# GLA level products over the later halves of the queries, packed two blocks to a bank, with the diagonal apart

## The chip, the cores and the metric

The kernel runs on one core of a Trainium2 chip. The metric is device time in microseconds of one execution. In the profile PE is TensorE's matmul, PEld its weight load, DVE is VectorE, ACT ScalarE, POOL GpSimd, and SP the queue that starts most DMA transfers.

## The reference

A two-layer decoder trunk on 512 tokens of width 1024, all in float32. Each layer has three mixers on one projection (differential attention, a short convolution, gated linear attention), an output projection, and a layer of 16384 single-neuron experts. The change concerns the gated linear attention (GLA): 4 heads with 32 key and 64 value channels, in chunks of 64 tokens.

```python
def step(state, inp):                      # one chunk of 64 tokens
    qi, ki, vi, ai = inp
    b = lax.cumsum(ai, axis=2)
    diff = b[:, :, :, None, :] - b[:, :, None, :, :]
    decay = jnp.exp(jnp.where(causal[:, :, None], diff, -jnp.inf))
    attn = jnp.sum(qi[:, :, :, None, :] * ki[:, :, None, :, :] * decay, axis=-1)
    o = jnp.einsum('bhij,bhje->bhie', attn, vi) + jnp.einsum('bhid,bhde->bhie', qi * jnp.exp(b), state)
    b_last = b[:, :, -1:, :]
    state = jnp.exp(b_last[:, :, 0, :, None]) * state + jnp.einsum(
        'bhjd,bhje->bhde', ki * jnp.exp(b_last - b), vi)
    return state, o
```

The decay differs for each key channel, so `attn` is not one plain product of queries and keys.

## The kernel before

Each layer runs `mixer` and then the expert stage. `mixer` projects the normalized tokens with slabs of 256 columns of w_in. A slab is loaded in four pieces (wraw, L242), split by ScalarE into a rounded part wh (L80) and by VectorE into the rest wl (L81), and multiplied in three passes (L75 to L77) into psp. Slabs are double-buffered. While TensorE works through the slabs of the attention's queries, keys and values, `mixer` draws pieces of `gla` from a generator: `fill(n)` advances it until the costs that it yields add up to n. For the queries and keys each slab has also a rotation on VectorE (the rope: rm and qkn, L413 to L418) and transposes on TensorE (rtr, L422). The framework then orders the instructions of each engine by its own list scheduling, and each engine executes its list in that order.

`gla` works with 128 partitions (4 heads of 32 key channels) and 512 tokens. After the cumulative decay b, the masked matrix `at` (keys in partitions; block, head and query along the row) is built in seven levels (`level`, L527 to L547). Level s = 32, 16, 8, 4, 2, 1 covers the pairs whose key lies in the earlier and whose query in the later half of the same block of 2s tokens. With r the decay at the middle of that block, d is exp(r - b) in the earlier half and exp(b - r) in the later one (ld, L534 to L536). Keys are multiplied by d (ks, L539), and so are the queries of all tokens, spread out by head in qbm so that one product forms all four heads (qs, L540). For each block of 128 tokens TensorE forms a product of 128 keys with 4 x 128 queries (pst, L545), and VectorE copies from it the entries that the mask of that level selects (L547). The level s = 0 is the diagonal, with plain gk and qbm. Half of each product's columns, those of queries in earlier halves, are never selected.

Between levels, `gla` transposes the decayed keys (trk, L562), forms the chunk updates (psu, L572) and the states S on VectorE (L574 to L578). At the end it forms qe (L590), which shares its buffer with qs, and for each block the outputs pg from states (L596, L597) and from `at` (L599), normalizes them and transposes them (htr, L479). The attention's scores are pss (L438).

PSUM pool psA has four banks, used by pst, rtr and trk among others.

Of the kernel before, what the change touches and what calls it, by code (L numbers as in the profile page):

```python
# [7 lines left out]
F32 = mybir.dt.float32  # L8
# [4 lines left out]
U32 = mybir.dt.uint32  # L13
AF = mybir.ActivationFunctionType
OP = mybir.AluOpType
# [4 lines left out]
P = 128  # L20
T = 512
TB = T // P
# [37 lines left out]
def bc(ap, pattern):  # L60
    return bass.AP(tensor=ap.tensor, offset=ap.offset, ap=[ap.ap[0]] + pattern)


class K:
# [418 lines left out]
    def gla(self, L, gq, gk, gv, sg, lr, mgh, mgl, gp):  # L483
        nc, tc, ins = self.nc, self.tc, self.ins
# [5 lines left out]
        ggain = gp.tile([P, 1], F32, name="ggain")  # L490
        for i in range(2):
            nc.sync.dma_start(ggain[64 * i:64 * i + 64], ins["gla_norm"][L].rearrange("(p o) -> p o", o=1))
        lmask = gp.tile([P, 7, P], U32, name="lmask")
        nc.sync.dma_start(lmask, ins["c_levels"].rearrange("l p i -> p l i"))
        bdmask = gp.tile([P, 256], F32, name="bdmask")
        nc.gpsimd.memset(bdmask, 0.0)
        qbm = gp.tile([P, TB, 4, P], F32, name="qbm")
        nc.gpsimd.memset(qbm, 0.0)
        for h in range(4):
            r = slice(32 * h, 32 * h + 32)  # L500
            nc.gpsimd.memset(bdmask[r, 64 * h:64 * h + 64], 1.0)
            nc.scalar.copy(qbm[r, :, h], gq[r].rearrange("p (n i) -> p n i", i=P))
        reset = gp.tile([P, T], F32, tag="ld", name="reset", bufs=2)
        nc.gpsimd.memset(reset, 1.0)
        nc.gpsimd.memset(reset.rearrange("p (n c) -> p n c", c=C)[:, :, 0:1], 0.0)
# [1 line left out]
        def tmp(name):  # L507
            return gp.tile([P, T], F32, tag="tmp", name=name, bufs=2)
# [10 lines left out]
        b = gp.tile([P, T], F32, name="b")  # L519
# [4 lines left out]
        at = gp.tile([P, TB, 4, P], F32, name="at")  # L524
        nc.gpsimd.memset(at, 0.0)

        def level(li, s):  # L527
            if s:
                n = T // (2 * s)
                d = gp.tile([P, T], F32, tag="ld", name="ld", bufs=2)  # L530
                dv = d.rearrange("p (n two s) -> p n two s", two=2, s=s)
                bv = b.rearrange("p (n two s) -> p n two s", two=2, s=s)
                r = bc(b[:, s - 1:T], [[2 * s, n], [0, s]])
                nc.vector.tensor_tensor(dv[:, :, 0], r, bv[:, :, 0], op=OP.subtract)  # L534
                nc.vector.tensor_tensor(dv[:, :, 1], bv[:, :, 1], r, op=OP.subtract)
                nc.scalar.activation(d, d, AF.Exp)  # L536
                ks = gp.tile([P, T], F32, tag="ks", name="ks", bufs=2)
                qs = gp.tile([P, TB, 4, P], F32, tag="qs", name="qs", bufs=1)
                nc.vector.tensor_tensor(ks, gk, d, op=OP.mult)  # L539
                nc.vector.tensor_tensor(qs, qbm, bc(d, [[P, TB], [0, 4], [1, P]]), op=OP.mult)  # L540
            else:
                ks, qs = gk, qbm
            for tb in range(TB):
                pst = self.psA.tile([P, 4, P], F32, tag="a", name="pst")
                nc.tensor.matmul(pst, ks[:, tb * P:tb * P + P], qs[:, tb].rearrange("p h i -> p (h i)"),  # L545
                                 start=True, stop=True)
                nc.vector.copy_predicated(at[:, tb], bc(lmask[:, li], [[0, 4], [1, P]]), pst)  # L547

        levels = [(li, s) for li, s in enumerate((32, 16, 8, 4, 2, 1, 0))]
        level(*levels[0])  # L550
        yield 5

# [4 lines left out]
                                op=OP.subtract)  # L557
# [6 lines left out]
        nc.scalar.copy(kdT, trk)  # L564
        yield 3
        level(*levels[1])
        yield 6
        S = gp.tile([P, NC - 1, 256], F32, name="S")
# [11 lines left out]
        for lv in levels[2:]:  # L580
            level(*lv)
            yield 6
        self.tap("at", at)
        eb = tmp("eb")
        nc.scalar.activation(eb, b, AF.Exp)
        qe = gp.tile([P, 2, T], F32, tag="qs", name="qe", bufs=1)
        nc.gpsimd.memset(qe, 0.0)
        for i in range(2):
            sl = lambda t: t.rearrange("p (n two c) -> p n two c", two=2, c=C)[:, :, i]
# [2 lines left out]
        for tb in range(TB):  # L592
            pg = self.psB.tile([P, 256], F32, tag="b", name="pg")
            t0 = tb * P
# [3 lines left out]
            for h in range(4):  # L598
                nc.tensor.matmul(pg[:, 64 * h:64 * h + 64], at[:, tb, h], gv[:, tb, 64 * h:64 * h + 64],  # L599
                                 start=False, stop=(h == 3))  # L600
# [407 lines left out]
def lay_out(inputs):  # L1008
    import numpy as np

    a = {n: np.asarray(v) for n, v in inputs.items()}
    L = DEPTH
    r = {}
    r["x"] = a["x"].reshape(T, D)
    r["positions"] = a["positions"].reshape(T)
    for n in ("norm_mix", "norm_ffn", "w_in", "lam_q1", "lam_k1", "lam_q2", "lam_k2", "diff_norm", "gla_w_gate2", "gla_b_gate", "gla_norm",
              "w_out", "norm_final"):
        r[n] = a[n]
    r["conv_w"] = a["conv_w"].reshape(L, 3, 2, P).transpose(0, 3, 2, 1)
    r["peer_w_q"] = a["peer_w_q"].reshape(L, KD, P, 16, P).transpose(0, 3, 2, 1, 4)  # L1020
    for n in ("peer_keys1", "peer_keys2"):
        r[n] = a[n].transpose(0, 2, 1)
    r["peer_u"] = a["peer_u"].reshape(L, NCH, P, KD, P).transpose(0, 1, 4, 3, 2)
    r["u_rows"] = a["peer_u"].reshape(L * NCH * P, D)
    r["v_rows"] = a["peer_v"].reshape(L * NCH * P, D)
    r["c_ident"] = np.eye(P, dtype=np.float32)
    j, i = np.arange(P)[:, None], np.arange(P)[None, :]
    xr = j ^ i
    r["c_levels"] = np.stack([((xr >= s) & (xr < 2 * s) & (i > j)) if s else (xr == 0)
                              for s in (32, 16, 8, 4, 2, 1, 0)]).astype(np.uint32)  # L1030
    return {n: np.ascontiguousarray(v) for n, v in r.items()}


# [14 lines left out]
```

## Time and profile before

| | us |
|---|---|
| median of 3 runs (lowest, highest) | 3073.7 (3073.36, 3074.85) |
| the profiled execution | 3068.26 |
| its span, first to last instruction | 3066.5 |
| TensorE busy in the span | 2996.6 |
| VectorE busy | 2470.3 |
| GLA of layer 0, from psz to the first attention score | 128.80 |
| GLA of layer 1, the same | 128.60 |

Runs are compared by the time of the whole execution; the profile gives one execution's span, 1.8 us shorter than its time. A busy TensorE may be one whose passes overlap: an instruction's recorded length includes time in which the next one already runs, so the pace is the distance between two starts.

### The profile page before, as it was taken

To read this page: it belongs to the slowest core of one execution; us is meant where nothing else is said; L and a number is where in the kernel's file an instruction comes from. 1 tells how busy PE (TensorE), PEld (TensorE's weight loads), DVE (VectorE), ACT (ScalarE), POOL (GpSimd) and SP (SyncE) were. 2 spreads that over 40 slices of the span, in tenths; PEclk is the share of its full clock that TensorE was granted. 3 is DMA by queue.
4 is the path that set the end of the run, shared out by engine and by line. 5 is a ranking of instruction groups with operands and counts; after the bars stand their busy time and mean duration, and the time that the engine had idled before them with its cause. 6 is when DMAs were issued, how large, how long until landed. Compare 5 with 4: busy or idle time off the path is not lost.

```text
span 3066.5 us, 45595 instructions
## 1 busy us (share of the span) xinstructions
PE 2996.6 (98%) x16742; PEld 2657.9 (87%) x16742; DVE 2470.3 (81%) x5079; ACT 1268.5 (41%) x1874; POOL 739.7 (24%) x543
## 2 busy tenths in 40 slices
PE   8999999999999999999999999999999999999998
PEld 7777889999999998788878788899998999988886
DVE  5777999987778887877766769999878877878777
ACT  5244346556333333333352433465553333323333
POOL 0000000222455544322100000002225555543221
PEclk9999999999999999999999999999999999999999
DMA  4112238799998888999722122478999888889996
GB/s 123 56 45 91 89 122 263 260 316 334 338 333 324 322 325 307 357 338 334 275 76 69 59 72 90 155 246 287 310 343 340 321 326 331 331 306 350 334 344 232
DMA packets 335664, 757.03 MB, mean 247 GB/s; under 512 B 30000, under 2 KB 192208, under 8 KB 331344
## 3 DMA queue, kind: packets, MB, share of 16 engines
q1 hardware_dynamic: 141904, 407.00, 37.1%
q0 software_dynamic: 73728, 268.47, 24.5%
q10 hardware_dynamic: 119808, 78.66, 8.2%
q8 instruction: 131, 2.15, 0.3%
q14 instruction: 93, 0.76, 0.1%
HBM read 673.28 MB, written 80.74 MB: 246 GB/s over the span
## 4 chain that ended last, share of the span: by engine, by line
PE 74%; issue 7%; DVE 7%; POOL 4%; DMA 3%; ACT 3%; ACTq 1%; SPq 0%; POOLq 0%; DVEq 0%
PE pv L77 9%; PE pv L75 9%; PE pv L76 9%; PE psh L75 8%; PE psh L77 8%; PE psh L76 8%; POOL row L715 4%; PE psp L77 2%; PE psp L76 2%; PE psp L75 2%; DMA row<-in_v_rows,idx 2%; PE psq L76 2%; PE psq L77 2%; PE psq L75 2%; PE pst L545 1%
## 5 line engine op out<-in xcount | busy, mean ns | idle before, releaser
L715 POOL DMA_INDIRECT row<-in_u_rows,idx x256 | 390.6, 1526 | 1315.9 <-DVE si L873 669.5
L75 PE MATMUL psh<-ahi,uh 128*128 128x384 f32 x2048 | 694.7, 339 | 10.3 <-ACT ht L645 10.3
L77 PE MATMUL psh<-ahi,ul 128*128 128x384 f32 x2048 | 689.6, 337 | 6.6 <-DVE ul L631 6.6
L76 PE MATMUL psh<-alo,uh 128*128 128x384 f32 x2048 | 688.8, 336 | 0.0
L75 PE MATMUL pv<-vh,wh 128*128 128x512 f32 x1536 | 598.1, 390 | 8.1 <-ACT wh L815 8.1
L77 PE MATMUL pv<-vh,wl 128*128 128x512 f32 x1536 | 601.2, 392 | 0.0
L76 PE MATMUL pv<-vl,wh 128*128 128x512 f32 x1536 | 600.3, 391 | 0.0
L715 POOL DMA_INDIRECT row<-in_v_rows,idx x256 | 331.5, 1295 | 601.5 <-DVE yacc L732 565.7
L630 ACT CAST uh<-uraw 128x1024 fp32r<-128x1024 f32 x288 | 302.5, 1053 | 322.0 <-PE psh L76 156.1
L631 DVE TENSOR_TENSOR ul<-uraw,uh 128x1024 fp32r<-128x1024 f32 x288 | 350.4, 1220 | 99.3 <-ACT uh L630 87.9
L75 PEld LDWEIGHTS psh<-ahi,uh 128*128 128x128 f32 x2048 | 387.0, 189 | 16.4 <-ACT ht L645 12.2
L77 PEld LDWEIGHTS psh<-ahi,ul 128*128 128x128 f32 x2048 | 386.8, 189 | 7.2 <-DVE ul L631 7.2
L76 PEld LDWEIGHTS psh<-alo,uh 128*128 128x128 f32 x2048 | 387.3, 189 | 4.1
L801 DVE TENSOR_TENSOR vl<-vraw,vh 128x1024 fp32r<-128x1024 f32 x256 | 312.6, 1221 | 83.2 <-issue 64.5
L645 ACT ACTIVATE ht<-psh 128x384 f32<-128x384 f32 x256 | 125.3, 489 | 612.4 <-PE psh L77 605.5
L75 PEld LDWEIGHTS pv<-vh,wh 128*128 128x128 f32 x1536 | 288.7, 188 | 67.5 <-ACT wh L815 10.5
L77 PEld LDWEIGHTS pv<-vh,wl 128*128 128x128 f32 x1536 | 289.0, 188 | 62.6 <-DVE wl L801 1.9
L76 PEld LDWEIGHTS pv<-vl,wh 128*128 128x128 f32 x1536 | 289.1, 188 | 59.4 <-DVE vl L801 1.0
L732 DVE SCALAR_TENSOR_TENSOR yacc<-row,wk,yacc 128x1024 f32<-128x1024 f32 x254 | 325.7, 1282 | 10.9 <-DMA row<-in_v_rows,idx 9.3
L723 DVE SCALAR_TENSOR_TENSOR gscr<-row,xg 128x1024 f32<-128x1024 f32 x256 | 312.4, 1220 | 13.2 <-DMA row<-in_u_rows,idx 11.6
L815 ACT CAST wh<-ht 128x384 fp32r<-128x384 f32 x256 | 130.7, 510 | 385.0 <-PE pv L76 229.5
L806 ACT CAST vh<-vraw 128x1024 fp32r<-128x1024 f32 x256 | 268.7, 1050 | 25.3 <-DMA vraw<-in_v_rows 24.5
(285 smaller groups left out, 4451.2 us busy)
## 6 DMA issues: line engine op xcount, KB each, us to landing
uraw<-in_peer_u SPq DMA_DIRECT2D x256, 512.0 KB
vraw<-in_v_rows SPq DMA_DIRECT2D x256, 512.0 KB
G<-stg ACTq DMA_DIRECT2D x48, 1024.0 KB
g<-G SPq DMA_DIRECT2D x32, 1536.0 KB
H<-ht ACTq DMA_DIRECT2D x144, 192.0 KB
ht<-H SPq DMA_DIRECT2D x144, 192.0 KB
wraw<-in_w_in SPq DMA_DIRECT2D x96, 256.0 KB
uraw<-in_peer_w_q SPq DMA_DIRECT2D x32, 512.0 KB
```

Source lines behind the costliest of these rows:

```text
L75: mm(ps, ah, bh, start=first, stop=False)
L76: mm(ps, ah, bl, start=False, stop=False)
L77: mm(ps, al, bh, start=False, stop=last)
L630: pin(nc.scalar.copy(hi, src))
L631: self.last = pin(nc.vector.tensor_tensor(lo, src, hi.bitcast(F32), op=OP.subtract))
L645: pin(nc.scalar.activation(hs[c], ps, AF.Gelu))
L715: nc.gpsimd.indirect_dma_start(out=r, out_offset=None, in_=ins[name], in_offset=bass.IndirectOffsetOnAxis(ap=idx[:, k:k + 1], axis=0))
L723: nc.vector.scalar_tensor_tensor(sc, r, 1.0, xg, op0=OP.mult, op1=OP.mult, accum_out=hd[:, k:k + 1])
L732: nc.vector.scalar_tensor_tensor(yacc, r, wk[:, k:k + 1], yacc, op0=OP.mult, op1=OP.add)
L801: self.last = pin(nc.vector.tensor_tensor(lo, src, hi.bitcast(F32), op=OP.subtract))
L806: pin(nc.scalar.copy(vh[c], vs[c]))
L815: pin(nc.scalar.copy(wh[c], hs[c]))
```

## The change

`level` now multiplies d only into the queries of the later halves: qs has 4 x 256 elements instead of 4 x 512 and two buffers. Each product has 4 x 64 columns, and two blocks share one bank of PSUM, from which one copy writes the later halves of both blocks into `at`; the masks hold only those columns. The level s = 0 is gone. In its place `diagonal` multiplies gq by gk on VectorE (qk), sums over each head's channels with four products with hsel, a matrix of zeros and ones with four columns (dots), and copies these sums, repeated along the row, into `at` where dmask selects the diagonal. It yields 3 instead of the 6 of a level, so the pieces of `gla` behind it are drawn one slab earlier. qe takes the new buffer form of qs.

```diff
-        lmask = gp.tile([P, 7, P], U32, name="lmask")
+        lmask = gp.tile([P, 6, P // 2], U32, name="lmask")
         nc.sync.dma_start(lmask, ins["c_levels"].rearrange("l p i -> p l i"))
+        dmask = gp.tile([P, P], U32, name="dmask")
+        nc.sync.dma_start(dmask, ins["c_diag"])
+        hsel = gp.tile([P, 4], F32, name="hsel")
+        nc.gpsimd.memset(hsel, 0.0)
...
-        qbm = gp.tile([P, TB, 4, P], F32, name="qbm")
+        qbm = gp.tile([P, 4, T], F32, name="qbm")
...
-            nc.scalar.copy(qbm[r, :, h], gq[r].rearrange("p (n i) -> p n i", i=P))
+            nc.gpsimd.memset(hsel[r, h:h + 1], 1.0)
+            nc.scalar.copy(qbm[r, h], gq[r])
...
-                qs = gp.tile([P, TB, 4, P], F32, tag="qs", name="qs", bufs=1)
-                nc.vector.tensor_tensor(ks, gk, d, op=OP.mult)
-                nc.vector.tensor_tensor(qs, qbm, bc(d, [[P, TB], [0, 4], [1, P]]), op=OP.mult)
-            else:
-                ks, qs = gk, qbm
+            qs = gp.tile([P, 4, T // 2], F32, tag="qs", name="qs", bufs=2)
+            nc.vector.tensor_tensor(ks, gk, d, op=OP.mult)
+            nc.vector.tensor_tensor(qs.rearrange("p h (n s) -> p h n s", s=s),
+                                    qbm.rearrange("p h (n two s) -> p h n two s", two=2, s=s)[:, :, :, 1],
+                                    bc(d[:, s:T], [[0, 4], [2 * s, n], [1, s]]), op=OP.mult)
+            m = P // (2 * s)
+            for t0 in range(0, TB, 2):
+                pst = self.psA.tile([P, 8, P // 2], F32, tag="a", name="pst")
+                for i in range(2):
+                    tb = t0 + i
+                    nc.tensor.matmul(pst[:, 4 * i:4 * i + 4], ks[:, tb * P:tb * P + P],
+                                     qs[:, :, tb * 64:tb * 64 + 64], start=True, stop=True)
+                nc.vector.copy_predicated(
+                    at[:, t0:t0 + 2].rearrange("p b h (n two s) -> p (b h) n two s", two=2, s=s)[:, :, :, 1],
+                    bc(lmask[:, li], [[0, 8], [s, m], [1, s]]), pst.rearrange("p g (n s) -> p g n s", s=s))
+
+        def diagonal():
+            qk = tmp("qk")
+            nc.vector.tensor_tensor(qk, gq, gk, op=OP.mult)
+            dots = self.psA.tile([P, TB, 4], F32, tag="a", name="dots")
             for tb in range(TB):
-                pst = self.psA.tile([P, 4, P], F32, tag="a", name="pst")
-                nc.tensor.matmul(pst, ks[:, tb * P:tb * P + P], qs[:, tb].rearrange("p h i -> p (h i)"),
-                                 start=True, stop=True)
-                nc.vector.copy_predicated(at[:, tb], bc(lmask[:, li], [[0, 4], [1, P]]), pst)
-
-        levels = [(li, s) for li, s in enumerate((32, 16, 8, 4, 2, 1, 0))]
+                nc.tensor.matmul(dots[:, tb], qk[:, tb * P:tb * P + P], hsel, start=True, stop=True)
+            for tb in range(TB):
+                nc.vector.copy_predicated(at[:, tb], bc(dmask, [[0, 4], [1, P]]), bc(dots[:, tb], [[1, 4], [0, P]]))
+
+        levels = [(li, s) for li, s in enumerate((32, 16, 8, 4, 2, 1))]
...
+        diagonal()
+        yield 3
...
-        qe = gp.tile([P, 2, T], F32, tag="qs", name="qe", bufs=1)
+        qe = gp.tile([P, 2, T], F32, tag="qs", name="qe", bufs=2)
```

The scheduler places some instructions elsewhere. TensorE's list differs from row 360 to row 1058 of layer 0 and in the same part of layer 1, and nowhere else; it has 17488 rows before and after. A row here is one line of an engine's list, in which equal neighbours are joined.

TensorE, levels s = 8 and 4 in layer 0 before (rows 477 to 481):

```order
L422 MATMUL rtr<-ident,qkn 128x128 x4
L545 MATMUL pst<-qs,ks 128x512
L572 MATMUL psu<-gv,kdT 128x256
L545 MATMUL pst<-qs,ks 128x512 x3
L77 MATMUL psp<-wh,alo 128x256
```

and the same place after (rows 478 to 482):

```order
L422 MATMUL rtr<-ident,qkn 128x128 x4
L552 MATMUL pst<-qs,ks 128x256 x2
L590 MATMUL psu<-gv,kdT 128x256
L552 MATMUL pst<-qs,ks 128x256 x6
L77 MATMUL psp<-wh,alo 128x256
```

Level s = 8 stood here alone, with s = 4 36 rows of psp later; now both stand together. The first level stands behind 89 rows of psp, counted from psz (row 270), where it stood behind 98, and the rows between it and the next rtr changed with it.

TensorE, the end of the levels before (rows 686 to 690), where the second pst is the diagonal:

```order
L422 MATMUL rtr<-ident,qkn 128x128 x4
L545 MATMUL pst<-qs,ks 128x512 x4
L545 MATMUL pst<-qbm,gk 128x512 x4
L76 MATMUL psp<-wl,ahi 128x256
L77 MATMUL psp<-wh,alo 128x256
```

and after (rows 684 to 688):

```order
L422 MATMUL rtr<-ident,qkn 128x128 x4
L552 MATMUL pst<-qs,ks 128x256 x4
L563 MATMUL dots<-hsel,qk 128x4 x4
L76 MATMUL psp<-wl,ahi 128x256
L77 MATMUL psp<-wh,alo 128x256
```

Behind these, 83 rows of psp stood before the first block's pg (L599 reads `at`); now 13 stand before it.

VectorE between the first half of the second slab's rope (qkn) and what precedes it, before (rows 176 to 187):

```order
L540 TENSOR_TENSOR qs<-qbm,ld 128x2048
L578 SCALAR_TENSOR_TENSOR S<-S,dec,um 128x256
L534 TENSOR_TENSOR ld<-b 128x64x4
L535 TENSOR_TENSOR ld<-b 128x64x4
L413 TENSOR_TENSOR rm<-qkn,cos 128x64
L414 TENSOR_TENSOR rm<-qkn,sin 128x64
L415 TENSOR_TENSOR rm<-qkn,sin 128x64
L416 TENSOR_TENSOR rm<-qkn,cos 128x64
L417 TENSOR_TENSOR qkn<-rm 128x8x8
L418 TENSOR_TENSOR qkn<-rm 128x8x8
L539 TENSOR_TENSOR ks<-gk,ld 128x512
L81 TENSOR_TENSOR wl<-wraw,wh 128x512 x3
```

and after, the rows ahead of that rope, which begins at row 181 (rows 170 to 180):

```order
L554 COPY_PREDICATED at<-lmask,pst 128x32x16
L544 TENSOR_TENSOR qs<-qbm,ld 128x1024
L554 COPY_PREDICATED at<-lmask,pst 128x32x16
L592 TENSOR_TENSOR S<-psu,bdmask 128x256
L595 TENSOR_TENSOR um<-psu,bdmask 128x256
L543 TENSOR_TENSOR ks<-gk,ld 128x512
L596 SCALAR_TENSOR_TENSOR S<-S,dec,um 128x256
L544 TENSOR_TENSOR qs<-qbm,ld 128x1024
L595 TENSOR_TENSOR um<-psu,bdmask 128x256
L81 TENSOR_TENSOR wl<-wraw,wh 128x512
L596 SCALAR_TENSOR_TENSOR S<-S,dec,um 128x256
```

Two qs of later levels and the first weight splits (wl) now stand ahead of that rope, where before the splits stood behind it.

## Rows read from the trace of the kernel before

**Rows 1.** The page, parts 1 and 4: busy time of each engine, and the chain by engine.
```profile
PE 2996.6 (98%) x16742; PEld 2657.9 (87%) x16742; DVE 2470.3 (81%) x5079; ACT 1268.5 (41%) x1874; POOL 739.7 (24%) x543
PE 74%; issue 7%; DVE 7%; POOL 4%; DMA 3%; ACT 3%; ACTq 1%; SPq 0%; POOLq 0%; DVEq 0%
```

**Rows 2.** Windows: length, then busy us (instructions) of PE, PEld, DVE, ACT, POOL; PEclk.
```profile
59.28:188.08 128.80, 124.03 (x795) 101.84 (x795) 89.08 (x214) 43.98 (x78) 2.80 (x3) 1.00 0.20 58
188.08:245.00 56.92, 55.48 (x282) 40.09 (x281) 46.80 (x144) 32.75 (x88) 0.00 (x0) 1.00 0.20 70
1582.00:1710.60 128.60, 124.06 (x795) 101.86 (x794) 88.94 (x214) 44.17 (x78) 2.82 (x3) 1.00 0.20 58
```

**Rows 3.** Waits of PE in 59.28:188.08: us in total, times, longest.
```profile
PE pst L545 <- DVE qs L540: 2.0, 1, 2.0
PE htr L479 <- DVE ho L471: 1.8, 2, 1.3
PE rtr L422 <- ACT wh L80: 0.4, 2, 0.2
PE rtr L422 <- DVE qkn L418: 0.2, 1, 0.2
```

**Rows 4.** Tile pst: instructions of both layers, ns min/median/max.
```profile
L545 PE MATMUL pst<-qs,ks x96: 592/592/697, 74.1 to 1662.5; 128*128 128x512 f32 x96
L545 PE MATMUL pst<-qbm,gk x16: 592/592/593, 140.3 to 1666.0; 128*128 128x512 f32 x16
L547 DVE COPY_PREDICATED at<-lmask,pst x56: 709/729/751, 75.2 to 1666.7; 128x512 f32<-128x512 uint32 x56
```

**Rows 5.** The chain, layer 0: start us, us, what (x instructions).
```profile
120.55 3.44 PE pst L545 x8
...
137.02 6.87 PE pst L545 x16
...
161.29 0.43 PE pg L596 x2
161.73 0.43 PE pg L597 x2
162.16 0.85 PE pg L599 x8
```

**Rows 6.** PE in order of time at the first level: start, us, instruction.
```profile
60.55 0.28 PE L76 MATMUL psp<-wl,ahi 128*128 128x256 f32 x1
...
71.81 0.28 PE L76 MATMUL psp<-wl,ahi 128*128 128x256 f32 x1
74.05 3.70 PE L545 MATMUL pst<-qs,ks 128*128 128x512 f32 x8 [1.96 <-DVE qs L540]
77.59 1.04 PE L422 MATMUL rtr<-ident,qkn 128*128 128x128 f32 x8
```

**Rows 7.** The chain at the first level, DVE pieces: start us, us between two starts.
```profile
69.91 0.14 DVE rm L414
71.20 0.60 DVE ks L539
71.79 2.20 DVE qs L540
...
74.60 0.34 DVE ld L534
...
76.18 0.65 DVE at L547
```

**Rows 8.** Line L535: DVE, all six levels of both layers, ns min/median/max.
```profile
L535 DVE TENSOR_TENSOR ld<-b x12: 409/417/436, 69.5 to 1637.7; 128x256 f32<-128x256 f32 x12
```

**Rows 9.** Tiles lmask and qe: the load on SP's queue, and POOL in order of time.
```profile
L494 SPq DMA_DIRECT2D lmask<-in_c_levels x2: 586/590/594, 17.2 to 1537.4; - x2
...
140.52 0.95 POOL L587 MEMSET qe<- 128x1024 f32 x1 [132.73 <-PE pst L545]
```

More of the change, by code (lines that the diff above doesn't have):

```diff
@@ L527, in level @@
         def level(li, s):
[L528 to L537, printed above, removed]
-                qs = gp.tile([P, TB, 4, P], F32, tag="qs", name="qs", bufs=1)
-                nc.vector.tensor_tensor(ks, gk, d, op=OP.mult)
-                nc.vector.tensor_tensor(qs, qbm, bc(d, [[P, TB], [0, 4], [1, P]]), op=OP.mult)
-            else:
-                ks, qs = gk, qbm
@@ L543, in level @@
-            for tb in range(TB):
-                pst = self.psA.tile([P, 4, P], F32, tag="a", name="pst")
-                nc.tensor.matmul(pst, ks[:, tb * P:tb * P + P], qs[:, tb].rearrange("p h i -> p (h i)"),
-                                 start=True, stop=True)
-                nc.vector.copy_predicated(at[:, tb], bc(lmask[:, li], [[0, 4], [1, P]]), pst)
-        levels = [(li, s) for li, s in enumerate((32, 16, 8, 4, 2, 1, 0))]
+            n = T // (2 * s)
+            halves = lambda t: t.rearrange("p (n two s) -> p n two s", two=2, s=s)
@@ new lines, in level @@
+            d = gp.tile([P, T], F32, tag="ld", name="ld", bufs=2)
+            dv, bv = halves(d), halves(b)
+            r = bc(b[:, s - 1:T], [[2 * s, n], [0, s]])
+            nc.vector.tensor_tensor(dv[:, :, 0], r, bv[:, :, 0], op=OP.subtract)
+            nc.vector.tensor_tensor(dv[:, :, 1], bv[:, :, 1], r, op=OP.subtract)
+            nc.scalar.activation(d, d, AF.Exp)
+            ks = gp.tile([P, T], F32, tag="ks", name="ks", bufs=2)
+            qs = gp.tile([P, 4, T // 2], F32, tag="qs", name="qs", bufs=2)
@@ L1028, in lay_out @@
     xr = j ^ i
-    r["c_levels"] = np.stack([((xr >= s) & (xr < 2 * s) & (i > j)) if s else (xr == 0)
-                              for s in (32, 16, 8, 4, 2, 1, 0)]).astype(np.uint32)
+    r["c_levels"] = np.stack([((xr >= s) & (xr < 2 * s) & (i > j))[:, (i[0] & s) > 0]
+                              for s in (32, 16, 8, 4, 2, 1)]).astype(np.uint32)
+    r["c_diag"] = (xr == 0).astype(np.uint32)
     return {n: np.ascontiguousarray(v) for n, v in r.items()}
```

## The prediction

> **What bounds the kernel now.** I read the page first. TensorE is busy for 98% of the span and carries 74% of the chain, VectorE 81% and 7% [rows 1]. The change touches only the gated linear attention (GLA), which each layer runs once, so I next took the stretch from its first product (psz) to the first attention score: 128.80 us in layer 0, 128.60 us in layer 1, with TensorE busy 124.03 and 124.06 us, VectorE 89.08, ScalarE 43.98, GpSimd 2.80 [rows 2]. TensorE leaves only 4.8 us there. The waits say the same: 4.4 us in all, the largest the 2.0 us before the first level product, which waits for qs [rows 3]. So in this stage time is TensorE's work plus a few short waits, and removed TensorE work should come off the end, provided that the others keep up.
>
> **What one product costs.** A fp32 product stands in the trace as two passes: 48 products of levels 0 to 5 (both layers) are 96 instructions, the 8 of the diagonal 16, and each is recorded with 592 ns [rows 4]. That length overlaps with the next pass, so I price by the distance from start to start, which the chain gives: 8 passes in 3.44 us and 16 in 6.87 us, 0.43 us for a pass over 512 columns. The passes of pg over 256 columns take 0.43 us for two, 0.215 each, and those over 64 columns 0.85 us for eight, 0.106 each [rows 5]. From 512 to 256 columns the price halves exactly; below that a floor near 0.106 us shows.
>
> **The change, TensorE.** Before, a layer issues 7 x 4 = 28 products, 56 passes x 0.43 = 24.1 us. After: 6 levels x 4 products x 2 passes = 48 passes of 256 columns x 0.215 = 10.3 us; and 4 diagonal products with 4 moving columns, 8 passes for which no row exists. Their lower bound is nothing, the nearest row is the 64-column pass, 0.106 us, so 0.85 us; the upper bound is the 256-column pass, 1.7 us. I take 0.85. Sum 11.2 us, so **12.9 us less per layer**, 25.8 us in both.
>
> The moving operand is now four runs of 64 columns and the masked half of each block. No row has that form; if it cost as much as an unbroken 512-column pass there would be only the diagonal's gain, and if it is as pg's, the full one. I take pg's, since it has the same width and type.
>
> The Trainium skill, "TensorE: Matmul & The Clock Gate", section "Back-to-back issue gap", gives a sustained 81 ns for 128 columns and 131 ns for 512, so that a quarter of the columns still costs 62%. On a line through both, a half costs 75%, an estimate from the page: 48 passes would take 15.4 us and the gain would be 7.9 us per layer, 16 us in all. The rows of this trace differ from it: 0.43 and 0.215 us [rows 5].
>
> **VectorE.** The copies fall from 28 to 16 of 512 elements each, at 0.65 us from start to start: 7.8 us less. qs falls from 2048 to 1024 elements; 512 elements take 0.60 us (ks) and 2048 take 2.20 [rows 7], so 1.04 ns per element and 1.13 us, 6 x 1.07 = 6.4 us less. qk adds one 512-element product, 0.60 us. VectorE sheds 13.6 us, about what TensorE sheds, so its share stays near 65%: (89.08 - 13.6) / (128.8 - 12.9). Copies and qs now step through memory in runs of s elements, down to one. Line L535 already does that for every s from 32 to 1 and takes 409 to 436 ns [rows 8], so I price runs at nothing; the other bound is below (rivals).
>
> **Edits priced at nothing.** qbm's four ScalarE copies keep their size. One more load (dmask) stands on SP's queue behind lmask, whose own takes 0.59 us there [rows 9]; behind it wait loads of w_in. TensorE is busy 124 of 128.8 us on work whose weights are already there, which hides it; without that cover it costs up to 0.6 us per layer. The five hsel fills on GpSimd run beside 2.80 us of work in 128.8. qe now waits for level 4 instead of 5, and its fill takes 0.95 us [rows 9], long before pg.
>
> **The new order.** Here is what may go wrong. (1) The first level: qs ends 1.07 us earlier, but TensorE now meets it after 89 projection passes instead of 98. Those come every (71.81 - 60.55) / 96 = 0.117 us [rows 6], so it arrives 1.05 us earlier too: the wait of 1.96 us stays. (2) The next queries' transposes (rtr, first half of the second slab). From the first level's pst, at 72.98 us, TensorE has two levels (3.44), 73 projection passes (8.6), three groups of four transposes at 0.44 (rtr x8 before trk start 0.88 apart [rows 6]; trk taken alike) and three psu of about 0.33: 14.3 us, to 87.3. VectorE must before that do ks of level 0 up to the rope, 38 instructions: eleven of 512 elements at 0.60 to 0.65, four qs at 1.13, eleven of 256 at about 0.35, twelve rope pieces at 0.14 [rows 7], 16.9 us from 71.2, to 88.1, because two weight splits (wl) and the next levels now stand ahead of that rope. TensorE then waits some 0.8 us; before, all its waits at rtr were 0.6 us [rows 3]. (3) At the end, pg of the first block follows 13 projection passes (1.5 us) behind the diagonal instead of 83 behind the last level; the diagonal's first copy takes 0.65 us plus its latency, so it is just in time, and if pg waits for all four copies, 1.2 us is added. I take 1 us per layer for all new waits; bounds 0 and 6.
>
> From TensorE's row 1059 of a layer on, and so in the whole expert stage, the order is the same row for row; what stands there shifts and keeps its length.
>
> **Sum.** Per layer 12.9 - 1 = 11.9 us, two layers 23.8. The profiled execution took 3068.3 us (span 3066.5), so 3044.5; it was 5.4 us shorter than the median of the runs shown, 3073.7, against which I forecast **3050 us**.
>
> **Rivals.**
> A. Passes don't halve, because a fixed cost or the broken operand keeps them long: at 0.32 us (midway between 0.215 and 0.43) the levels take 15.4 us and the gain is 7.9 per layer, 3058 us. Against it: the halving in [rows 5]. For it: no row has four runs. The page's line above comes to the same time.
> B. The new order makes waits: VectorE, with splits ahead of level work, is late at each of the eight rope transposes of a layer by about 0.8 us as computed for one of them. That gives back 6 us per layer: 3062 us. For it: point (2). Against it: VectorE is idle for 40 of 128.8 us [rows 2], mostly in the second half, where it catches up.
> C. No change: the attention and output stage behind is set by something else than TensorE, and the time saved becomes a wait there: 3074. Against it: there TensorE is busy 55.48 of 56.92 us [rows 2].
> D. Slower: scattered runs make VectorE the bound. It is busy 75.5 us after the change if runs are free; TensorE needs 116. It decides at +40 us per layer, and the kernel is slower at +53, that is if the 16 copies and 6 qs (17.2 us) took four times as long: at five times VectorE needs 144 us, 15 more than the stage takes now, 3105 us. [Rows 8] speak against any such factor.
>
> **Chances.** Forecast 0.70 (its own range 3045 to 3055), A 0.09, B 0.14, C 0.04, D 0.03. The fastest case is the full 25.8 us with the waits at the transposes and heads halved, 3045. The range 3045 to 3062 holds the forecast, A and most of B. A measurement of this kernel can tell 0.2%, 6 us, from no change: faster 0.93, same 0.04, slower 0.03.
>
> **What would show it.** pst passes 0.215 us from start to start and dots near 0.106; the stretch from psz to the first score near 113 us: 11.9 less, and another 4 because 17 projection passes of 512 columns (0.23 us each, twice the 256-column pace) now stand behind that score; VectorE near 75 us there; qs near 1.2 us and copies still near 0.73 us as recorded. A is seen in pst's pace, B in waits of rtr or pg for VectorE, D in copies that grow as s shrinks. The prediction is wrong if the stretch gets shorter so and the span doesn't.

## The result and the profile after

The changed kernel takes 3043.8 us (median of 6 runs, 3041.24 to 3052.66), the kernel before 3074.27 beside it (6 runs, 3068.8 to 3077.99). The ratio is 0.9906, 95% interval 0.989 to 0.9921, or 28.9 us less (24.3 to 33.8: one minus the ratio, times 3074.27). In a second comparison the ratio was 0.99 (0.9885 to 0.9916). The forecast was 3050, with 3044.5 against the profiled execution; the profiled execution after took 3044.03.

The page, parts 1 and 4, answers to [rows 1]:

```profile
PE 2971.3 (98%) x16742; PEld 2659.7 (87%) x16742; DVE 2443.7 (80%) x5057; ACT 1268.9 (42%) x1874; POOL 736.2 (24%) x553
PE 79%; DVE 6%; issue 4%; ACT 4%; DMA 3%; POOL 2%; ACTq 1%; SPq 0%; POOLq 0%; DVEq 0%
```

TensorE lost 25.3 us of work and VectorE 26.6, and TensorE still carries the chain. The windows from psz to the first score, and the one behind it, answer to [rows 2]:

```profile
60.88:172.20 111.32, 107.87 (x777) 99.36 (x777) 75.41 (x202) 44.78 (x78) 2.80 (x3) 0.98 0.23 67
172.20:229.10 56.90, 55.25 (x275) 40.27 (x273) 42.81 (x137) 28.12 (x79) 0.00 (x0) 1.00 0.17 60
1570.40:1681.70 111.30, 107.91 (x776) 99.19 (x776) 75.39 (x202) 44.69 (x78) 2.80 (x3) 0.98 0.23 67
```

The stretch is 17.5 us shorter in layer 0 and 17.3 in layer 1, but 18 more projection passes now stand behind the first score (the prediction counted 17). A fairer stretch runs from psz to the first product of the expert stage (psq): the work in it is the same but for the change. Its windows in both layers, of before and then of after:

```profile
59.28:297.40 238.12, 231.14 (x1331) 182.83 (x1331) 169.76 (x461) 96.40 (x200) 2.80 (x3) 1.00 0.19 59
1582.00:1820.00 238.00, 231.27 (x1331) 182.85 (x1331) 169.62 (x461) 96.71 (x200) 2.82 (x3) 1.00 0.19 59
```

```profile
60.88:286.30 225.42, 219.54 (x1331) 183.74 (x1331) 156.62 (x450) 96.59 (x200) 2.80 (x3) 0.99 0.20 63
1570.40:1796.00 225.60, 219.77 (x1331) 183.46 (x1331) 156.70 (x450) 96.49 (x200) 2.80 (x3) 0.99 0.19 63
```

That is 12.7 and 12.4 us less per layer, 25.1 in both. The span of the profiled execution is 24.2 us shorter, so the gain was made here. TensorE is busy 11.6 and 11.5 us less, VectorE 13.1 and 12.9. One column is new: PEclk is 0.99 and not 1.00.

The waits of PE in 60.88:172.20 answer to [rows 3]:

```profile
PE pst L552 <- DVE qs L544: 1.9, 1, 1.9
PE htr L479 <- DVE ho L471: 0.7, 2, 0.5
PE rtr L422 <- ACT wh L80: 0.2, 1, 0.2
PE rtr L422 <- DVE qkn L418: 0.2, 1, 0.2
```

Together 3.0 us, where it was 4.4 in layer 0. The tiles pst, dots and qs answer to [rows 4, 7]:

```profile
L552 PE MATMUL pst<-qs,ks x96: 379/379/634, 74.6 to 1641.8; 128*128 128x256 f32 x96
L554 DVE COPY_PREDICATED at<-lmask,pst x24: 697/726/1397, 75.8 to 1642.5; 128x512 f32<-128x512 uint32 x24
L563 PE MATMUL dots<-hsel,qk x16: 169/252/253, 132.5 to 1642.7; 128*128 128x4 f32 x16
L565 DVE COPY_PREDICATED at<-dmask,dots x8: 716/727/810, 134.1 to 1645.5; 128x512 f32<-128x512 uint32 x8
L544 DVE TENSOR_TENSOR qs<-qbm,ld x12: 1207/1218/1235, 73.3 to 1616.9; 128x1024 f32<-128x1024 f32 x12
```

The longest copy took 1397 ns, which the median hides. Line L554 in layer 0 by time, first the levels s = 32 to 4 and then s = 2 and 1:

```profile
L554 DVE COPY_PREDICATED at<-lmask,pst x8: 697/710/734, 75.8 to 102.8; 128x512 f32<-128x512 uint32 x8
L554 DVE COPY_PREDICATED at<-lmask,pst x4: 1284/1338/1393, 117.0 to 132.9; 128x512 f32<-128x512 uint32 x4
```

All these copies write 512 elements, but those of the last two levels write runs of two and of one element into `at`, and take nearly twice as long. Layer 1 shows the same (698 to 741, and 1285 to 1397 ns).

And the chain of layer 0, which gives the pace as [rows 5] did:

```profile
74.59 2.50 PE pst L552 x8
82.59 1.73 PE pst L552 x8
...
130.91 1.73 PE pst L552 x8
132.64 0.79 PE dots L563 x8
135.08 0.97 PE pg L619 x8
```

Eight passes in 1.73 us are 0.216 each, half of before; a dots pass takes 0.79 / 8 = 0.099 us. Only the first level is slower: 2.50 us for its eight passes (3.27 in layer 1). Windows of 2 us there, both layers:

```profile
74.00:76.00 2.00, 1.41 (x6) 1.25 (x7) 2.00 (x5) 0.09 (x1) 0.00 (x0) 0.99 0.00 0
76.00:78.00 2.00, 2.00 (x9) 1.68 (x8) 1.67 (x4) 0.56 (x2) 0.00 (x0) 0.50 0.00 0
78.00:80.00 2.00, 2.00 (x13) 2.00 (x13) 1.56 (x2) 1.09 (x3) 0.00 (x0) 0.66 0.00 0
80.00:82.00 2.00, 2.00 (x20) 2.00 (x19) 1.91 (x10) 2.00 (x5) 0.00 (x0) 1.00 0.00 0
...
1584.00:1586.00 2.00, 1.92 (x6) 1.58 (x7) 1.61 (x5) 0.61 (x1) 0.00 (x0) 0.66 0.03 8
1586.00:1588.00 2.00, 2.00 (x9) 1.61 (x7) 1.32 (x3) 0.02 (x1) 0.00 (x0) 0.50 0.00 0
1588.00:1590.00 2.00, 2.00 (x18) 2.00 (x18) 2.00 (x5) 1.52 (x3) 0.00 (x0) 0.99 0.00 0
```

Behind the wait for qs the granted clock falls to 0.50, the 1.2 GHz level, and is back within some 4 us. Before, with the same wait of 1.96 us [rows 6], the clock was 1.00 over the whole stretch [rows 2].

### The profile page after: what moved, and what is told of

It reads as the page before. It is cut to its first block, busy times and chain, and to the rows that moved or that the text cites. A ratio compares the mean times of both kernels' runs of the same rounds, so it can differ in the third digit from the quotient of the medians.

```text
span 3042.3 us, 45583 instructions
## 1 busy us (share of the span) xinstructions
PE 2971.3 (98%) x16742; PEld 2659.7 (87%) x16742; DVE 2443.7 (80%) x5057; ACT 1268.9 (42%) x1874; POOL 736.2 (24%) x553
## 4 chain that ended last, share of the span: by engine, by line
PE 79%; DVE 6%; issue 4%; ACT 4%; DMA 3%; POOL 2%; ACTq 1%; SPq 0%; POOLq 0%; DVEq 0%
PE pv L77 10%; PE pv L76 10%; PE pv L75 10%; PE psh L75 9%; PE psh L77 9%; PE psh L76 9%; PE psp L77 2%; PE psp L76 2%; PE psp L75 2%; PE psq L76 2%; PE psq L77 2%; PE psq L75 2%; POOL row L735 2%; DMA row<-in_v_rows,idx 1%; ACTq L789 1%
## 5 line engine op out<-in xcount | busy, mean ns | idle before, releaser
L75 PEld LDWEIGHTS psh<-ahi,uh 128*128 128x128 f32 x2048 | 387.1, 189 | 16.2 <-ACT ht L665 11.9
L826 ACT CAST vh<-vraw 128x1024 fp32r<-128x1024 f32 x256 | 268.7, 1050 | 26.6 <-DMA vraw<-in_v_rows 24.5
```

Source lines behind the costliest of these rows:

```text
L75: mm(ps, ah, bh, start=first, stop=False)
L826: pin(nc.scalar.copy(vh[c], vs[c]))
```

## The experiments

The theory: TensorE's passes set the time of this stretch, and the halved products made the gain. The rivals: VectorE's relief made it, or the new order did. The first four kernels ran side by side.

**The packed levels alone.** The diagonal goes back to a full product.

```diff
-            qk = tmp("qk")
-            nc.vector.tensor_tensor(qk, gq, gk, op=OP.mult)
-            dots = self.psA.tile([P, TB, 4], F32, tag="a", name="dots")
             for tb in range(TB):
-                nc.tensor.matmul(dots[:, tb], qk[:, tb * P:tb * P + P], hsel, start=True, stop=True)
+                pst = self.psA.tile([P, 4, P], F32, tag="a", name="pst")
+                nc.tensor.matmul(pst, gk[:, tb * P:tb * P + P], qbm[:, :, tb * P:tb * P + P], start=True, stop=True)
```

> The packed levels alone: the diagonal is formed as before, by a full product of 512 columns per token block (8 passes a layer), and copied in under the diagonal's mask. If TensorE's passes decide, a layer has 48 passes x 0.215 + 8 x 0.43 = 13.7 us of them, against 24.1 before: 10.3 less, 20.6 us in two layers, and with 1 to 2 us a layer for waits or a lower clock at the first level about 17 to 19 us faster than before. If it is VectorE's relief that counts, the gain is that of the whole change or more, 24 to 30 us, since VectorE sheds the same 12 copies and half of qs and does not even form qk.

Measured: 3050.81 us, ratio 0.9933 (0.992 to 0.9947), 20.6 us less (16.3 to 24.6). TensorE's passes expected 17 to 19, VectorE's relief 24 to 30; the measured value lies between, its interval holds the first and touches the second. From psz to psq layer 1 took 226.8 us, 11.2 less than before, with the clock at 1.00; layer 0, where the clock fell, 228.6.

**The diagonal apart, alone.** The levels are those of before, seven masks are loaded and the last serves as dmask.

```diff
-        levels = [(li, s) for li, s in enumerate((32, 16, 8, 4, 2, 1, 0))]
+        levels = [(li, s) for li, s in enumerate((32, 16, 8, 4, 2, 1))]
...
             level(*lv)
             yield 6
+        diagonal()
+        yield 3
```

> The separate diagonal alone, with the level products of before. TensorE's passes: 48 x 0.43 + 8 x 0.106 = 21.5 us a layer against 24.1, so 2.6 less, about 5 us faster in all (0.2%). VectorE sheds nothing and gets qk, 0.6 us a layer: if VectorE decides, no gain, or 1 us slower. The granted clock in the stretch of the first level should stay 1.00 if the halved passes are what lets it fall, and drop if the new diagonal or the new load has to do with it.

Measured: 3068.44 us, ratio 0.9982 (0.9972 to 0.9992), 5.5 us less (2.5 to 8.6), as TensorE's passes say. The two parts, 20.6 and 5.5, add up to 26.1, near the whole. The clock fell in layer 0 here too, with the full 512-column products, so the halved passes are not what lets it fall.

**Every level product twice.** The second product writes the same values again.

```diff
-                for i in range(2):
+                for i in (0, 1, 0, 1):
```

> The changed kernel with every level product issued twice (the second overwrites the first with the same values). TensorE gets 48 passes x 0.215 = 10.3 us a layer more, VectorE nothing. If TensorE decides, 20.6 us of the gain are given back: about 4 to 9 us faster than before. If VectorE's relief decides, the gain stays as in the changed kernel, 24 to 30 us.

Measured: 3065.54 us, ratio 0.9973 (0.9962 to 0.9984), 8.3 us less (4.9 to 11.7). Of the gain some 20 us are given back though VectorE keeps its relief. TensorE's passes expected 20.6. The new order doesn't make the gain either: this kernel has nearly the same one (the first level stands behind 89 passes of psp, and the first pg 14 passes behind dots, against 13).

**VectorE's work twice.** The level copies are made twice, and qs is filled first with the earlier halves.

```diff
+            nc.vector.tensor_tensor(qs.rearrange("p h (n s) -> p h n s", s=s),
+                                    qbm.rearrange("p h (n two s) -> p h n two s", two=2, s=s)[:, :, :, 0],
+                                    bc(d, [[0, 4], [2 * s, n], [1, s]]), op=OP.mult)
...
+                for _ in range(2):
```

> The changed kernel with VectorE's work of before put back: each level copy is made twice, and the earlier halves of the queries are multiplied into qs first and then overwritten by the later halves. VectorE gets about 13.6 us a layer more, TensorE nothing. If TensorE decides and VectorE was hidden, the gain stays but for the later first qs (1.1 us a layer) and some waits: 18 to 24 us faster than before. If VectorE's relief made the gain, nothing or 5 us of it is left.

Measured: 3055.68 us, ratio 0.9951 (0.9938 to 0.9964), 15.1 us less (11.1 to 19.1). That is below the 18 to 24 expected, and far above nothing: neither theory as stated. The windows from psz to psq:

```profile
59.00:288.40 229.40, 218.83 (x1332) 182.73 (x1332) 172.78 (x469) 96.55 (x200) 2.81 (x3) 1.00 0.20 62
1574.50:1804.50 230.00, 219.16 (x1332) 182.72 (x1332) 172.81 (x469) 96.83 (x200) 2.80 (x3) 1.00 0.20 61
```

TensorE works no more than in the changed kernel (218.83 us) but idles 10.6 us. Its waits from 1560 to 1690 us, layer 1:

```profile
PE rtr L422 <- DVE qkn L418: 2.1, 2, 1.9
PE pst L555 <- DVE qs L547: 2.0, 1, 2.0
PE psp L76 <- DVE wl L81: 1.8, 1, 1.8
PE pg L623 <- DVE at L569: 0.9, 1, 0.9
PE htr L479 <- DVE ho L471: 0.8, 2, 0.5
```

These are the waits of the prediction's rival B: with TensorE faster, VectorE's late ropes, splits and copies are met. VectorE's relief doesn't make the gain, but with this load about half of the gain is lost to such waits. The load is more than that of before: VectorE is busy 172.78 us here, 169.76 before, and the slow copies of the last two levels, doubled here, are among the difference. So half is probably more than the old load alone would have cost.

**The first level's products later.** The next three kernels try to remove the wait for qs. Here the products and copies of the first level are written behind the next slab.

```diff
-        level(*levels[0])
+        first = level(*levels[0])
         yield 5
 
+        products(*first)
```

> The changed kernel with the first level's products and copies written behind the next projection slab (its VectorE part stays where it is); TensorE then meets them after 112 projection passes and 8 transposes behind psz instead of 89 passes, about 3.6 us later. If the 1.95 us wait for qs is a matter of order, it goes, and with it the fall of the granted clock behind it: 1.95 + about 1.7 us a layer, so 4 to 7 us faster than the changed kernel, 28 to 36 us faster than before. Rival: the wait moves to the transposes of the queries (they now come ahead of the first level and need the rope on VectorE), and the time is that of the changed kernel within 2 us; the clock then falls there.

Measured: 3044.43 us, ratio 0.9906 (0.989 to 0.9922): no gain on the changed kernel, as the rival said. The wait moved to the transposes, and no fall of the clock followed, which the rival had expected there. From psz to psq its layers take 224.2 and 224.1 us, as a layer of the changed kernel does where the clock stays up (224.2, below). PE's waiting instruction in each layer:

```profile
71.66 0.63 PE L422 MATMUL rtr<-ident,qkn 128*128 128x128 f32 x4 [2.05 <-DVE qkn L418]
...
1580.45 0.63 PE L422 MATMUL rtr<-ident,qkn 128*128 128x128 f32 x4 [2.05 <-DVE qkn L418]
```

**The diagonal first.**

```diff
+        diagonal()
         level(*levels[0])
         yield 5
...
-        diagonal()
-        yield 3
```

> The changed kernel with the diagonal formed ahead of the first level instead of behind the last. TensorE has the 8 small passes and 109 projection passes ahead of the first level instead of 89: it comes about 3.2 us later, qs about 0.6 us later (qk) or 3.2 (if the four diagonal copies stand ahead too). If qk alone stands ahead, the wait shrinks to nothing and the clock stays at its higher level: 4 to 7 us faster than the changed kernel. If the copies stand ahead too, nothing changes at that place. At the end pg no longer follows the diagonal by 13 projection passes, which the trace of the changed kernel shows as no wait, so no gain from there.

Measured: 3049.93 us, ratio 0.9927 (0.9912 to 0.9942), 22.4 us less, 6 to 8 worse than the changed kernel: a miss. The wait at the first level is gone, but dots now wait 1.25 us for qk, and behind that the clock falls in both layers. From psz to psq the layers take 227.7 and 228.1 us, some 2.4 more than in the changed kernel, whose clock fell in both layers too. So the fall alone doesn't explain the loss: the transposes of the outputs (htr) now wait 1.9 and 2.2 us in all for VectorE's ho, against 0.7 and 0.5, and TensorE is busy 1.4 and 1.1 us longer. Why, no run takes apart. The two windows of layer 0 behind the wait:

```profile
70.00:72.00 2.00, 2.00 (x12) 2.00 (x12) 2.00 (x4) 0.00 (x0) 0.00 (x0) 0.52 0.00 0
72.00:74.00 2.00, 2.00 (x13) 2.00 (x13) 2.00 (x10) 0.63 (x1) 0.00 (x0) 0.63 0.00 0
```

**Both moves**, diagonal() placed ahead of products(*first).

> Both moves at once: the diagonal behind the next slab, then the first level's products and copies. As for the later products alone, 4 to 7 us faster than the changed kernel if the wait for qs goes; the diagonal's place adds nothing to it. If the queries' transposes now wait for the rope, the gain is gone and the time is the changed kernel's.

Measured: 3054.54 us, ratio 0.9936 (0.9921 to 0.9951), 19.7 us less: a miss as well. The transposes wait 1.99 and 1.88 us, and in layer 1 once more, 2.22 us, with the clock at 0.50 behind that; the layers take 226.9 and 232.0 us. Here too htr waits over 2 us for ho in each layer.

**One and a half slabs later.** The first level's products and the transposes both move behind enough projection passes.

```diff
                     for tbs, ps in down(256 * i):
-                        self.rope_T(ps, (qT, kT)[i // 2], i % 2, tbs, qp)
-                    fill(10 + 10.5 * (i + 1))
+                        turn()
+                        turn = self.rope_T(ps, (qT, kT)[i // 2], i % 2, tbs, qp)
+                        if i == 1:
+                            fill(20.5)
+                    if i:
+                        fill(10 + 10.5 * (i + 1))
```

rope_T returns its four transposes as turn(), which is called one pair of blocks later; the first level's products stand behind a yield as above.

> The changed kernel with the first level's products one and a half projection slabs later and each pair's transposes of the queries and keys one projection pair (48 passes) later. By the places: TensorE has 96 projection passes from psz to the first transposes (about 72.5 us where psz is at 61; the rope ended at 72.2 in the changed kernel) and another 48 and 8 transposes to the first level (78.7 us; qs ended at 74.6). Both long waits should go: no wait over 1 us in the stretch, no fall of the granted clock in either layer. That is 1.95 and about 1.7 us a layer, 4 to 7 us faster than the changed kernel run beside it. Rival: VectorE is late at the next place (levels 1 and 2, or the recurrence), and the wait is found there; then within 2 us of the changed kernel.

Measured: 3042.23 us, ratio 0.989 (0.9872 to 0.9907), 33.8 us less (28.6 to 39.4). The changed kernel ran beside it:

> The changed kernel once more, on the same chip as the half-slab variant, for a comparison side by side and for a second look at the granted clock behind the 1.95 us wait. If the fall belongs to this program, it shows in both layers again; if it is a matter of the execution (it fell behind such a wait in 5 of 12 places so far, in kernels with either form of the levels), it may be there or not. Time as before, 24 to 30 us faster than the kernel before.

Measured: 3045.68 us, ratio 0.99 (0.9885 to 0.9916). The variant's median is the lowest of all, but the two intervals overlap, so that it beats the changed kernel is not shown by the times. The trace shows it where it was made. Windows from psz to psq, of the variant and then of the changed kernel beside it:

```profile
61.20:284.20 223.00, 218.04 (x1331) 181.92 (x1331) 156.38 (x450) 95.94 (x200) 2.80 (x3) 1.00 0.21 63
1571.00:1794.10 223.10, 217.87 (x1332) 182.16 (x1332) 156.56 (x450) 95.71 (x200) 2.81 (x3) 1.00 0.21 63
```

```profile
60.40:284.60 224.20, 218.41 (x1332) 182.50 (x1332) 156.36 (x450) 96.64 (x200) 2.80 (x3) 1.00 0.21 63
1570.20:1795.50 225.30, 219.50 (x1331) 183.61 (x1331) 156.60 (x450) 96.56 (x200) 2.80 (x3) 0.99 0.21 63
```

The variant's longest wait of TensorE from psz to the first score is 1.0 us (psu for S), and its layers are 1.2 and 2.2 us shorter: less than the 4 to 7 expected in all. Part of the removed wait came back, 0.9 us at psu for VectorE's S, as the rival said, and 0.4 us at pst for ScalarE's qT. And a fall costs less here than the 1.7 us that was assumed. The changed kernel itself shows that: the same program, nearly the same wait (1.96 and 1.83 us), and the clock fell in layer 1 only. There TensorE's busy time is 1.1 us longer, and so is the stretch. In the first three experiments, where one layer of the two had a fall, the price was nearer to the 1.7: TensorE's busy time from psz to psq differs between the layers by 1.6 to 1.8 us.

**The mask from the identity.** The load of dmask is gone.

```diff
-        dmask = gp.tile([P, P], U32, name="dmask")
-        nc.sync.dma_start(dmask, ins["c_diag"])
+        dmask = self.ident.bitcast(U32)
```

> The changed kernel with the diagonal's mask taken from the identity matrix that the program holds already (its ones, read as integers, are as good as any value that isn't zero), so that the load of dmask is gone from SP's queue. The instructions of all other engines stand as in the changed kernel. If the load is hidden, as the prediction priced it, the time is that of the changed kernel within 1 us a layer; if it delays the projection weights behind it, 0.6 us a layer comes off, which shows in the stretch from psz to the next layer's work and hardly in the time.

Measured: 3048.48 us, ratio 0.9904 (0.9887 to 0.9922), the same as the changed kernel beside it. SP's queue from 17 us, of the changed kernel and then of this one:

```profile
18.25 0.59 SPq L494 DMA_DIRECT2D lmask<-in_c_levels  x1
18.88 0.54 SPq L496 DMA_DIRECT2D dmask<-in_c_diag  x1
19.47 0.43 SPq L337 DMA_DIRECT2D cw<-in_conv_w  x1
28.23 3.85 SPq L242 DMA_DIRECT2D wraw<-in_w_in  x4
```

```profile
18.28 0.59 SPq L494 DMA_DIRECT2D lmask<-in_c_levels  x1
18.91 0.54 SPq L337 DMA_DIRECT2D cw<-in_conv_w  x1
28.22 3.88 SPq L242 DMA_DIRECT2D wraw<-in_w_in  x4
```

The weights are asked for at 28.2 us with the load or without it, and from psz to psq the layers take 225.5 and 225.6 us, as in the changed kernel's first execution (225.4 and 225.6), whose clock fell in both layers too: the load cost nothing.

## Why the prediction was right, step by step

**The bound.** TensorE sets the time of the stretch, as the prediction read it. The expectations drawn from its passes came near for the levels, the diagonal and the doubled products (17 to 19, 5, and 4 to 9 us less than before; measured 20.6, 5.5 and 8.3, the first above its range, which lies within its interval).

**The price of a pass.** 0.215 us was forecast and 0.216 came; four runs of 64 columns cost what an unbroken 256 do. On the line that the prediction drew, as an estimate, through the figures of the Trainium skill, "TensorE: Matmul & The Clock Gate", section "Back-to-back issue gap", it would have been 0.32; the trace differs from that, and so from rival A, which set the same price. For dots, 0.106 was taken and 0.099 measured. Where the clock stayed up, TensorE lost 231.14 - 218.41 = 12.7 us a layer; the step said 12.9.

**VectorE.** 75.5 us of busy time were forecast and 75.41 came, to the first score. To psq, over the same work, VectorE shed 13.1 and 12.9 us where the step said 13.6. The step priced runs of s elements at nothing, from L535. For qs that holds: 1207 to 1235 ns at every s. For the copies it doesn't: at s = 2 and 1 they take 1284 to 1397 ns instead of 697 to 741. The prediction's sign of rival D, copies that grow as s shrinks, is there, in four copies of a layer at under twice the time. D needed four to five times in all copies and qs, so as a forecast of the time it is out; the slow copies were hidden because TensorE sets the time.

**Edits at nothing.** The mask's load is shown to be free; qe and hsel delayed nothing that the waits list.

**The new order.** (1) The wait for qs stayed, 1.95 us, as said. (2) The 0.8 us at the second slab's transposes didn't come: there is no wait there, and none over 0.22 us at any rtr of the stretch. (3) pg waited for nothing. The 1 us a layer for new waits was thus wrong in kind: the waits fell by 1.4 us in layer 0, and a loss that the prediction did not know, the lower clock behind the wait for qs, took 1.1 us where it struck. Net the layer lost 12.7 and 12.4 us instead of 11.9; that the two are so near is in part luck.

**Rivals B and C.** B's waits exist, as the kernel with VectorE's work doubled shows; in the changed kernel, where VectorE has shed 13 us a layer, they are absent. C failed: the stage behind kept its waits (pss for e, 1.4 us, before and after).

**The sum.** Against the profiled execution it was right: 3044.5 forecast, 3044.03 measured. The step that failed is the carrying over to the median. The profiled execution of before lay 5.4 us below the median of its runs, and the prediction added that to the result; the profiled execution after lies at its median (3044.03 and 3043.8). So 3050 was 6 us too high, and the measured median lies 1.2 us under the range of 3045 to 3062.

By the medians the gain is 29 to 31 us, by the traces 25; the executions of one kernel differ by more than that difference (3041 to 3053, 3066 to 3082 us), and what makes up those 4 to 6 us is settled only in part. The rest of the program, the span without the two stretches from psz to psq, took 2590 us before and 2591 after, but 2593 and 2598 in the second execution of the changed kernel and in the one with the identity's mask. So the two profiled executions compared here were shorter there than the other two. And the longer executions have the lower granted clock: of 43 of before, run beside the experiments, the 17 with a mean clock of 0.994 or more have spans of 3064 to 3074 us, the 10 with 0.992 or less 3074 to 3081. The profiled one had 0.994. That the clock makes the whole difference is not shown.

## What to carry to other kernels

Where one engine is busy for nearly all of a stretch, price a removed product from the distance between two starts of that shape in the same trace, and compare stretches that hold the same work. Ask also what the other engine would do if it kept its old load: here it was hidden before, and with 3 us a layer more than that load it cost half of the gain after. Look at the longest instruction of a line and not at the median alone: here four copies of a layer took nearly twice the time of the others, and the median showed nothing. A short wait that reordering seems able to remove can belong to a chain on another engine, as here; it then shows up at the next instruction that needs this chain, unless enough independent work is put ahead of all of them.

## What was not expected of the hardware

TensorE's clock can fall to its 1.2 GHz level behind a single short wait in an otherwise full stream, and it isn't the program alone that decides. Of 20 places with the long wait at the first level, or at the first transposes where it moved there (1.8 to 2.05 us; two in each of ten profiled executions), the clock fell behind 8: none of 2 before, 2 and then 1 of 2 in two executions of the changed kernel, 2 with the identity's mask, 1 each in the first three experiments, none with VectorE's work doubled, with the later products or with both moves. With the diagonal first it fell behind a wait of 1.25 us, in both layers. Nor is it the wait's length alone: with VectorE's work doubled, two further waits of 1.8 to 2.1 us in each layer had no fall behind them. What decides it stays open. A fall lasted 3.5 to 7 us here and cost 1.1 us in the changed kernel; only the variant whose longest wait there is 1.0 us and three kernels with longer waits were free of it.

VectorE's predicated copy of 512 fp32 elements out of PSUM took 0.70 to 0.74 us when it wrote runs of 32 to 4 elements, and 1.28 to 1.40 us with runs of 2 and 1. Two of its other instructions step through memory in runs of s too and kept their pace at every s: qs, which reads them, 1.21 to 1.24 us, and L535 before the change, which writes them, 0.41 to 0.44 us [rows 8]. Why the copy slows down and they don't stays open.
